# The first layer's output projection as seven quarter products, with its early weights in idle value buffers

## The chip, the core and the metric

The kernel runs on one core of one Trainium2 chip. The metric is device time in microseconds (us) of one execution; lower is better. The engines are TensorE (PE, matrix products), VectorE (DVE), ScalarE (ACT), GpSimd (POOL) and SyncE (SP, which issues most DMAs). They run asynchronously, each through its own instruction list in a fixed order, and wait for each other by semaphores. An instruction that waits holds up all that stands behind it on its engine.

## What is computed

An encoder trunk of two layers over 512 tokens of width 1024. Layer 0 mixes tokens by a neighbourhood attention, layer 1 by a latent attention; each has 16 heads, a SiLU gate z on the branch, an output projection, a residual add, and a gated embedding with a second 1024x1024 product.

```
def mixer_na(xn, w_in, rpb, w_out):
    q, k, v, z = jnp.split(xn @ w_in, 4, axis=-1)
    o = neighbourhood_attention(q, k, v, rpb)          # heads split and joined
    return (o.reshape(B, S, hd) * jax.nn.silu(z)) @ w_out
...
for each layer:  x = x + mixer(rmsnorm(x));  x = x + p * sigmoid(rmsnorm(x) @ gate)
```

All is fp32. A product is made of three terms on high and low parts (hi*hi, lo*hi, hi*lo), each a chain of matmuls on 128x128 by 128x512 tiles. A weight piece of 128x1024 is loaded raw, ACT copies its high part, and POOL or DVE subtracts to make its low part.

## The kernel before

Work is written with a scheduler that fixes the order on each engine from the dependences; pools of buffers (tags with a number of copies) decide when a load may start, and an instruction can be told to stand behind another (`issue_after`).

- **First attention** (about 100 to 241 us). `attend(j, also)` handles head pair j: scores, softmax, transposes, value products; `gated` multiplies the pair's output u by z on POOL and splits it into `oh` and `ol`. In each of the 16 heads `sum_step` issues one DMA of POOL's queue that adds two quarters of a gate weight in DRAM: 8 for the first layer's gate, 8 for the second's. The last three z products (`NLATE`) run between the last heads.
- **Output projection** (`out_proj`, 222 to 276 us). Two halves n of the columns by four token tiles t: eight products of 24 matmuls. Weights come by `load_w`; low parts go to POOL, or for every second piece to DVE. As soon as a product is added to the residual `r`, `turn_h` scales it, transposes it and hands it to `keep_half`, which makes the gate's operands.
- **Gate** (`gate_seven`, 276 to 317 us). Seven quarter products (Strassen's scheme with sums of weights and of operands) in the order 1, 7, 2, 6, 5, 3, 4, each of 24 matmuls. `prep(p)` loads and splits its two weight pieces; POOL makes all their low parts (L796).
- **Second layer.** The same with the latent attention (401 to 555 us); there POOL normalises each softmax tile `ex` (L1056) before PE transposes it.

Between projection and gate, raw weights share three `wraw` buffers, high and low parts three of `whi` and `wlo` each and ten of `w4`. PSUM has banks by tags T, O, S and mm, two each.

## Time and profile before

| | |
|---|---|
| median of 3 runs | 653.7 us (652.97 to 653.79) |
| the profiled execution | 653.56 us, of it 651.5 us span, mean granted PE clock 0.995 |
| PE busy | 640.2 us, 98% |
| ACT, DVE, POOL busy | 453.4, 427.7, 408.4 us |
| first attention's last value product | starts its successor at 241.49 us |
| output projection and gate | to about 276 us, to about 317 us |

Busy time of PE is the time in which at least one matmul is under way. A window row gives for a stretch of the span the busy time and the count of each engine. A group row gives line, engine, operation, tiles and shape, then busy time and mean duration in ns, then the idle time right before its instructions and what ended it. A timeline row gives start, duration and, in brackets, the idle time before.

### The profile page before, as it was taken

The page shows a single profiled execution, that of the slowest core. Times are in us where ns is not written, and L with a number is a line of the kernel's source. Part 1 is how long each engine was busy: PE and PEld are TensorE (multiplying, and loading weights), DVE is VectorE, ACT ScalarE, POOL GpSimd, SP SyncE. Part 2 cuts the span into 40 slices and gives each one's busy share as a digit, 9 for nine tenths or more (in the row PEclk, how much of TensorE's full clock was granted, in tenths as well). Part 3 has the DMA queues.
Part 4 walks back from the last instruction along what each step waited for, and adds up shares of the span by engine and source line. Part 5 has one row for each costly group of instructions (what it writes and reads, how often), then busy time and mean ns, then how long its engine had stood idle before and what let it go on. Part 6 is the DMA issues. An engine that isn't in the chain of part 4 may idle for free.

```text
span 651.5 us, 9980 instructions
## 1 busy us (share of the span) xinstructions
PE 640.2 (98%) x3299; PEld 541.9 (83%) x3299; DVE 427.7 (66%) x886; ACT 453.4 (70%) x903; POOL 408.4 (63%) x371
## 2 busy tenths in 40 slices
...
GB/s 326 355 124 306 217 66 179 263 205 217 229 209 217 239 178 342 147 154 188 224 140 102 78 109 156 32 75 24 49 50 66 65 84 112 229 292 126 193 65 162
DMA packets 46131, 107.41 MB, mean 165 GB/s; under 512 B 4736, under 2 KB 17792, under 8 KB 46080
## 3 DMA queue, kind: packets, MB, share of 16 engines
...
## 4 chain that ended last, share of the span: by engine, by line
PE 83%; POOL 1%; ACT 1%; DVE 0%; DMA 0%; issue 0%; POOLq 0%
PE ps_mm L123 27%; PE ps_S L123 10%; PE ps_mm L959 7%; PE ps_T L155 6%; PE ps_T L851 5%; PE ps_O L1071 5%; PE ps_mm L851 3%; PE ps_S L851 3%; PE ps_O L608 2%; PE ps_T L123 2%; PE ps_O L123 2%; PE ps_mm L909 2%; PE ps_T L301 2%; PE ps_T L596 2%; PE ps_S L909 1%; PE ps_S L559 1%
## 5 line engine op out<-in xcount | busy, mean ns | idle before, releaser
L101 POOL TENSOR_TENSOR wwlo<-wraw,wwhi 128x1024 fp32r<-128x1024 f32 (+5 forms) x68 | 122.3, 1810 | 93.5 <-ACT wwhi L100 41.9
L796 POOL TENSOR_TENSOR wlo<-wraw,whi 128x512 fp32r<-128x512 f32 x56 | 72.7, 1331 | 22.3 <-ACT whi L794 20.2
L1056 POOL TENSOR_TENSOR ex<-ex,rc 128x512 f32<-128x512 f32 x64 | 66.2, 1043 | 26.6 <-DVE rc L1055 22.5
L100 ACT ACTIVATE wwhi<-wraw 128x1024 fp32r<-128x1024 f32 (+5 forms) x71 | 55.1, 799 | 34.3 <-PE ps_mm L123 18.9
L1054 ACT ACTIVATE ex<-ps_S,mx 128x512 f32<-128x512 f32 x64 | 44.0, 687 | 12.6 <-DVE mx L1052 10.9
L1052 DVE TENSOR_REDUCE mx<-ps_S 128x1 f32<-128x512 f32 x64 | 43.7, 683 | 8.4 <-PE ps_S L123 7.7
L582 POOL TENSOR_TENSOR ex<-ex,rc 128x128 f32<-128x128 f32 (+1 forms) x64 | 37.5, 701 | 17.7 <-DVE rc L578 17.5
L112 DVE TENSOR_TENSOR pt_lo<-ps_T,pt_hi 128x512 fp32r<-128x512 f32 x64 | 43.1, 680 | 7.1 <-ACT pt_hi L110 6.7
L110 ACT ACTIVATE pt_hi<-ps_T 128x512 fp32r<-128x512 f32 x64 | 37.7, 594 | 3.4 <-PE ps_T L155 3.0
L155 PE MATMUL ps_T<-ident,ex 128*128 128x128 f32 x256 | 38.3, 272 | 0.0
L155 PEld LDWEIGHTS ps_T<-ident,ex 128*128 128x128 f32 x256 | 31.5, 140 | 7.5
L123 PE MATMUL ps_mm<-xh,wwhi 128*128 128x512 f32 x120 | 33.7, 404 | 0.0
L221 DVE TENSOR_TENSOR u<-ps_O,u 64x512 f32<-64x512 f32 x32 | 21.9, 685 | 17.7 <-ACT u L220 17.2
L576 ACT ACTIVATE ex<-ex,mx 128x128 f32<-128x128 f32 (+1 forms) x64 | 30.2, 473 | 4.2 <-DVE mx L565 4.1
L123 PE MATMUL ps_mm<-xl,wwhi 128*128 128x512 f32 x120 | 31.9, 395 | 0.0
L794 ACT ACTIVATE whi<-wraw 128x1024 fp32r<-128x1024 f32 x28 | 29.3, 1057 | 3.2 <-DMA wraw<-sum 2.4
L123 PE MATMUL ps_mm<-xh,wwlo 128*128 128x512 f32 x120 | 31.1, 394 | 0.0
L123 PE MATMUL ps_S<-ke,qe 96*128 96x512 f32 x96 | 28.9, 407 | 0.3 <-DMA qe<-rl 0.3
L123 PE MATMUL ps_S<-ko,qo 128*128 128x512 f32 x96 | 28.9, 409 | 0.0
L959 PE MATMUL ps_mm<-cT,wwhi 128*128 128x512 f32 x94 | 27.7, 393 | 0.0
L220 ACT ACTIVATE u<-ps_O 64x512 f32<-64x512 f32 x32 | 18.9, 591 | 12.0 <-PE ps_O L608 8.8
L225 POOL TENSOR_TENSOR u<-u,z 128x512 f32<-128x512 f32 x16 | 22.6, 1412 | 7.5 <-DVE u L221 7.5
...
## 6 DMA issues: line engine op xcount, KB each, us to landing
...
wraw<-na_qk SPq DMA_DIRECT2D x16, 512.0 KB, 4.9
wraw<-sum SPq DMA_DIRECT2D x16, 512.0 KB, 3.3
...
wraw<-gate SPq DMA_DIRECT2D x12, 512.0 KB, 3.3
wraw<-na_v SPq DMA_DIRECT2D x10, 512.0 KB, 3.4
...
wraw<-na_o SPq DMA_DIRECT2D x8, 512.0 KB, 4.8
```

Source lines behind the costliest of these rows:

```text
L100: nc.scalar.activation(hi[:, c], raw[:, c], AF.Copy)
L101: f = lambda e, c=c: e.tensor_tensor(out=lo[:, c], in0=raw[:, c], in1=hi[:, c].bitcast(F32), op=ALU.subtract)
L110: self.last_copy = self.act.activation(hi, src, AF.Copy, scale=scale)
L112: self.dve.tensor_tensor(out=lo, in0=src, in1=hi.bitcast(F32), op=ALU.subtract)
L123: last = self.last_mm = nc.tensor.matmul(out, l, r, start=i == 0, stop=i == n - 1)
L155: self.last_mm = self.nc.tensor.transpose(t[:, i * P:(i + 1) * P], b, self.ident)
L796: nc.gpsimd.tensor_tensor(out=lo[:, o], in0=raw[:, o], in1=hi[:, o].bitcast(F32), op=ALU.subtract)
L851: mm = nc.tensor.matmul(ps, l, r, start=j == 0 and p in banks, stop=j == 11 and p in (2, 3, 4), skip_group_check=True)
L959: self.last_mm = nc.tensor.matmul(PS[key], *terms[i], start=i == 0, stop=i == len(terms) - 1)
L1052: nc.vector.reduce_max(mx, sp, axis=AX.X, negate=True)
L1054: nc.scalar.activation(ex, sp, AF.Exp, bias=mx, accum_out=sm)
L1056: nc.gpsimd.tensor_tensor(out=ex, in0=ex, in1=rc.to_broadcast([P, S]), op=ALU.mult)
```

## The change

The first layer's output projection becomes `out_seven`: seven quarter products in the order 1, 7, 2, 4, 6, 5, 3, each of two token tiles with 12 matmuls. Products 2, 4, 5 and 3 accumulate on the banks of 1, 7, 6 and 6. Each result is added to or subtracted from one to three halves of the residual tiles. `gated_seven` multiplies u into z and forms sums and differences of z's halves on DVE: those for products 1 and 7 (head pairs 0 to 3) and 2 and 4 (pairs 4 to 7) become the operands `oh`, `ol`; those for 6, 5 (`Y`) and 3 (`Y3`) are split by ACT and DVE in `out_seven`. The sums of its weights (products 4 to 7) are made in DRAM in the first eight heads, the gate's in the other eight; the second layer's gate sums move into the second attention, one in each of heads 1 to 8, behind a normalisation.

`piece_of` loads one weight piece, 14 in all. `places` says where it goes: `w` is the ring of three, `v` the `w4` ring (now 8), `0` and `1` are two of the first attention's value buffers, now in a pool `seam`, that are free once their values are used. Products 1 and 7 are loaded from head pair 5 on. All low parts are POOL's but the second pieces of products 2 and 4, which DVE makes. The residual loads move into `out_seven`, behind `gp`. Transposes of odd tiles use bank O, the last late z bank S. The gate's order becomes 1, 7, 6, 2, 5, 3, 4, and `keep_mixed` makes its operands.

The orders below are taken behind the last attention head. First PE. Before, at the matmuls behind the last value product (`ww` is the fourth weight piece, `oh_1001` and `ol_1003` the operands of head pairs 4 to 7):

```order
L123 MATMUL ps_mm<-wwhi,ol_1002 128x512 x2
L123 MATMUL ps_mm<-wwlo,oh_1000 128x512 x2
L123 MATMUL ps_mm<-wwhi,oh_1001 128x512 x2
L123 MATMUL ps_mm<-wwhi,ol_1003 128x512 x2
L123 MATMUL ps_mm<-wwlo,oh_1001 128x512 x2
L123 MATMUL ps_S<-wwlo,oh_1001 128x512 x2
L123 MATMUL ps_S<-wwhi,ol_1003 128x512 x2
L123 MATMUL ps_S<-wwlo,oh_1001 128x512 x2
L123 MATMUL ps_mm<-ww_2617,oh_1001 128x512 [waits Activation_49]
L123 MATMUL ps_mm<-ww_2617,oh_1001 128x512
L123 MATMUL ps_mm<-ww_2617,ol_1003 128x512
L123 MATMUL ps_mm<-ww_2617,ol_1003 128x512 [waits Pool_49]
```

And now, from the last two value products (`ps_O`) on; `ps_mm` is product 7, `ps_T` product 2 on product 1's bank, `oh_1008` the operands of head pairs 4 to 7:

```order
L617 MATMUL ps_O<-ph,Q_510 128x256
L617 MATMUL ps_O<-pl,Q_510 128x256
L824 MATMUL ps_mm<-whi,oh_1007 128x512 x2
L824 MATMUL ps_mm<-whi,ol_1009 128x512 x2
L824 MATMUL ps_mm<-wlo,oh_1007 128x512 x2
L824 MATMUL ps_mm<-whi,oh_1007 128x512 x2
L824 MATMUL ps_mm<-whi,ol_1009 128x512 x2
L824 MATMUL ps_mm<-wlo,oh_1007 128x512 x2
L824 MATMUL ps_mm<-whi,oh_1007 128x512 x2
L824 MATMUL ps_mm<-whi,ol_1009 128x512 x2
L824 MATMUL ps_mm<-wlo,oh_1007 128x512 x2
L824 MATMUL ps_T<-whi,oh_1008 128x512 [waits DVE_49,Activation_49]
```

Before, 26 matmuls stand between the last value product and the first row that waits for the last head's operand; now 18 stand between it and product 2, whose first matmul waits for DVE and ACT. DVE's list at that place now (`Yl` is a low part of a Y operand, `wlo` the low part of product 2's second piece, the rows with `ps_T` are the adds of product 1; the last two read its first tile):

```order
L760 TENSOR_TENSOR z<-z 128x256 [waits DVE_49]
L802 TENSOR_TENSOR Yl<-z,Yh 128x512 [waits Activation_49]
L752 TENSOR_TENSOR wlo<-wraw,whi 128x512 [waits DMAHW7_49,Activation_49]
L752 TENSOR_TENSOR wlo<-wraw,whi 128x512
L833 TENSOR_TENSOR r<-r,ps_T 128x512 [waits DMAHW4_49]
L760 TENSOR_TENSOR z<-z 128x256 [waits Pool_49]
L833 TENSOR_TENSOR r<-r,ps_T 128x512 [waits DMAHW5_49]
L805 TENSOR_TENSOR Y_2687<-z,Y_2687 128x256 [waits Activation_49]
L833 TENSOR_TENSOR r<-r,ps_T 128x512 [waits DMAHW6_49]
L831 TENSOR_TENSOR r<-ps_T,r 128x512
```

Before, DVE had at that place only the last head's `u` and two low parts of weights. The second place is ACT and SP. ACT before, from the last head's evacuation `u<-ps_O` (L220) on:

```order
L220 ACTIVATE u<-ps_O 64x512 [waits PE_49]
L228 ACTIVATE oh_1001<-u 128x512 [waits Pool_49]
L100 ACTIVATE ww_2617<-wraw 128x1024 [waits DMAHW5_49]
L100 ACTIVATE ww_2777<-wraw 128x1024 [waits DMAHW6_49]
L100 ACTIVATE ww_2783<-wraw 128x1024 [waits DMAHW7_49]
L100 ACTIVATE ww_2789<-wraw 128x1024 [waits DMAHW5_49]
L100 ACTIVATE ww_2795<-wraw 128x1024 [waits DMAHW6_49]
```

And now, from the same evacuation (L227) on; `w_2737` is product 6's first piece, the two `whi` are product 2's:

```order
L227 ACTIVATE u<-ps_O 64x512 [waits PE_49]
L750 ACTIVATE w_2737<-wraw 128x1024 [waits DMAHW2_49]
L769 ACTIVATE oh_1008<-z 128x512 [waits Pool_49]
L750 ACTIVATE whi<-wraw 128x1024 [waits DMAHW6_49]
L801 ACTIVATE Yh<-z 128x512 [waits DVE_49]
L750 ACTIVATE whi<-wraw 128x1024 [waits DMAHW7_49,Activation_49]
L804 ACTIVATE Y_2687<-z 128x256 [waits DVE_49]
```

A weight's high part now stands between the evacuation and the last head's operand. SP before, around the residual loads:

```order
L99 DMA wraw<-na_o 128x1024 [waits DMAHW2_49,DVE_49,Activation_49]
L99 DMA wraw<-na_o 128x1024 [waits DMAHW3_49,Pool_49]
L1251 DMA r<-x 128x1024 [waits DMAHW0_49,PE_49]
L1251 DMA r<-x 128x1024 [waits DMAHW1_49,PE_49]
L1251 DMA r<-x 128x1024 x2
L148 DMA gp<-ple_norm 128x1024 [waits DMAHW4_49]
L99 DMA wraw<-na_o 128x1024 [waits DMAHW5_49,DVE_49]
L99 DMA wraw<-na_o 128x1024 [waits DMAHW6_49,Pool_49]
```

And now; `sumout_106` holds the weights of product 4, `sumout_108` of product 6:

```order
L748 DMA wraw<-sumout_106 128x1024 [waits DMAHW0_49,Activation_49,Pool_49]
L748 DMA wraw<-sumout_108 128x1024 [waits DMASW6_49,DMAHW1_49,DVE_49,Activation_49]
L155 DMA gp<-ple_norm 128x1024 [waits DMAHW3_49,DMASW1_49,PE_49]
L794 DMA r<-x 128x1024 [waits DMAHW4_49]
L794 DMA r<-x 128x1024
L794 DMA r<-x 128x1024 [waits DMAHW6_49]
L794 DMA r<-x 128x1024 [waits DMAHW7_49]
L748 DMA wraw<-sumout_108 128x1024 [waits DMAHW2_49,Activation_49,Pool_49]
```

The residual loads have moved behind product 4's second and product 6's first piece; the first of these waits for POOL, the second for DVE. The third place is POOL, before, from the last but one pair's `u` on:

```order
L225 TENSOR_TENSOR u<-u,z 128x512 [waits DVE_49]
L229 TENSOR_TENSOR ol_1003<-u,oh_1001 128x512 [waits Activation_49]
L101 TENSOR_TENSOR wwlo<-wraw,wwhi 128x1024 [waits DMAHW3_49,PE_49,Activation_49]
L225 TENSOR_TENSOR u<-u,z 128x512 [waits DVE_49]
L229 TENSOR_TENSOR ol_1003<-u,oh_1001 128x512 [waits Activation_49]
L101 TENSOR_TENSOR ww_2778<-wraw,ww_2777 128x1024 [waits DMAHW6_49,Activation_49]
L101 TENSOR_TENSOR ww_2790<-wraw,ww_2789 128x1024 [waits DMAHW5_49,PE_49,Activation_49]
```

And now; the first `wlo` is product 4's first piece, `w_2737` product 6's first, the second `wlo` product 2's first:

```order
L759 TENSOR_TENSOR z<-u,z 128x512 [waits DVE_49]
L752 TENSOR_TENSOR wlo<-wraw,whi 128x512 [waits DMAHW0_49,PE_49,Activation_49]
L752 TENSOR_TENSOR wlo<-wraw,whi 128x512
L770 TENSOR_TENSOR ol_1010<-z,oh_1008 128x512 [waits Activation_49] x2
L759 TENSOR_TENSOR z<-u,z 128x512 [waits DVE_49]
L752 TENSOR_TENSOR w_2737<-wraw,w_2737 128x512 [waits DMAHW2_49,PE_49,Activation_49]
L752 TENSOR_TENSOR w_2737<-wraw,w_2737 128x512
L770 TENSOR_TENSOR ol_1010<-z,oh_1008 128x512 [waits Activation_49]
L752 TENSOR_TENSOR wlo<-wraw,whi 128x512 [waits DMAHW6_49,PE_49,Activation_49]
L752 TENSOR_TENSOR wlo<-wraw,whi 128x512
```

The low part of product 4 waits for PE: its buffer was read last by the late z product of the last head pair. Product 6's low part has moved ahead of the last head's operand `ol`.

The diff:

```diff
-                l, step = divmod(j, 4)
-                if step == 0:
-                    self.quarters(l)
-                attend(j, lambda e: self.sum_step(l, 2 * step + e))
+                key = (("out", 0), ("gate", 0))[j // 4]
+                if j == 5:
+                    self.places = list("01wwvvw01vvwwv") + list("vw0v1vwwvvw0v1")
+                    self.out_early(None, 0, oT)
+                attend(j, lambda e: self.sum_step(key, 2 * (j % 4) + e))
...
             late = range(8 - NLATE, 8)
             zs.update(self.z_phase(a["na_z"], xT, late, self.last_exp.ins))
             for j in late:
-                self.gated(U[j], zs[j], oT, j)
+                gate(U[j], zs, oT, j)
...
+    def sum_step(self, key, i):
 
         p, src, add = ((7, "f", 0), (6, 1, 0), (7, 3, 1), (4, 2, 0), (6, 7, 1), (5, 1, 0), (4, 6, 1), (5, "f", 1))[i]
-        src = self.sums[layer][src] if src in (6, 7) else self.quarter[layer][src]
-        self.nc.gpsimd.dma_start(self.sums[layer][p], src, accum_op=ALU.add if add else ALU.bypass, max_dma_last_dim=1024)
+        src = self.sums[key][src] if src in (6, 7) else self.quarter[key][src]
+        self.nc.gpsimd.dma_start(self.sums[key][p], src, accum_op=ALU.add if add else ALU.bypass, max_dma_last_dim=1024)
+
+    def piece_of(self, pool, key, p, c, after=None, rest=None):
+        place = self.places.pop(0)
+        src = self.quarter[key][p] if p < 4 else self.sums[key][p]
+        raw = self.wp.tile([P, 1024], F32, name="wraw", tag="wraw", bufs=3)
+        if place in "01":
+            both = self.seam.tile([P, 2, 1024], F32R, name="w" + place, tag=f"Q{place}0", bufs=1)
+            hi, lo = both[:, 0, :], both[:, 1, :]
+        else:
+            q, n, tags = (self.wp, 3, ("whi", "wlo")) if place == "w" else (pool, self.wxn, ("w4", "w4"))
+            hi, lo = (q.tile([P, 1024], F32R, name=n0, tag=t, bufs=n) for n0, t in zip(("whi", "wlo"), tags))
+        self.last_load = nc.sync.dma_start(raw, src[c * P:(c + 1) * P])
+        with self.tc.issue_after(after.ins) if after else nullcontext():
+            self.act.activation(hi, raw, AF.Copy)
+        for o in (slice(0, S), slice(S, 2 * S)):
+            (rest or nc.gpsimd).tensor_tensor(out=lo[:, o], in0=raw[:, o], in1=hi[:, o].bitcast(F32), op=ALU.subtract)
+        return hi, lo
+
+    def gated_seven(self, u, zs, oT, j):
+
+        nc = self.nc
+        z = zs[j]
+        nc.gpsimd.tensor_tensor(out=z, in0=u, in1=z, op=ALU.mult)
+        sub = lambda o, x, y: nc.vector.tensor_tensor(out=o, in0=x, in1=y, op=ALU.subtract)
+        g, k = divmod(j, 4)
+        hi, lo = (oT[s][g][:, k, :] for s in range(2))
+        if g == 0:
+            sub(u[:, HI], z[:, LO], z[:, HI])
+            for x, c in ((z, LO), (u, HI)):
+                nc.scalar.activation(hi[:, c], x[:, c], AF.Copy)
+                nc.gpsimd.tensor_tensor(out=lo[:, c], in0=x[:, c], in1=hi[:, c].bitcast(F32), op=ALU.subtract)
+            return
+        nc.scalar.activation(hi, z, AF.Copy)
+        nc.gpsimd.tensor_tensor(out=lo, in0=z, in1=hi.bitcast(F32), op=ALU.subtract)
+        y = zs[k]
+        sub(y[:, HI], y[:, HI], z[:, HI])
+        sub(y[:, LO], y[:, LO], y[:, HI])
+        sub(z[:, LO], z[:, LO], y[:, LO])
+
+    def out_early(self, pool, layer, oT):
+
+        key = "out", layer
+        self.W = {}
+        self.oT = oT
+        for p in (1, 7):
+            self.W[p] = [self.piece_of(pool, key, p, c) for c in range(2)]
+
+    def out_seven(self, pool, layer, zs, res, after, last_mm):
+
+        nc = self.nc
+        key = "out", layer
+        oT, W = self.oT, self.W
+        order = (1, 7, 2, 4, 6, 5, 3)
+        C = {}
+        prep = lambda p: W.__setitem__(p, [self.piece_of(pool, key, p, c, rest=nc.vector if c and p in (2, 4) else None)
+                                           for c in range(2)])
+        for t in range(NT):
+            nc.sync.dma_start(res[t], self.a["x"][t] if layer == 0 else self.spill[t])
+        for p in order[2:4]:
+            prep(p)
+        Y = [self.bigtile(f"Y{s}") for s in "hl"]
+        Y3 = self.bigtile("Y3")
+        y3 = [Y3[:, 2 * s:2 * s + 2, :].rearrange("p a (b c) -> p (a b) c", b=2) for s in range(2)]
+        for k in range(4):
+            nc.scalar.activation(Y[0][:, k, :], zs[k], AF.Copy)
+            nc.vector.tensor_tensor(out=Y[1][:, k, :], in0=zs[k], in1=Y[0][:, k, :].bitcast(F32), op=ALU.subtract)
+        for k in range(4):
+            nc.scalar.activation(y3[0][:, k, :], zs[4 + k][:, LO], AF.Copy)
+            nc.vector.tensor_tensor(out=y3[1][:, k, :], in0=zs[4 + k][:, LO], in1=y3[0][:, k, :].bitcast(F32),
+                                    op=ALU.subtract)
+        src = {1: ([x[0] for x in oT], 0), 7: ([x[0] for x in oT], 256), 2: ([x[1] for x in oT], 0),
+               4: ([x[1] for x in oT], 256), 6: (Y, 0), 5: (Y, 256), 3: (y3, 0)}
+        banks = {1: "T", 7: "mm", 6: "S"}
+        home = {2: 1, 4: 7, 5: 6, 3: 6}
+        mm = last_mm
+        for n, p in enumerate(order):
+            if 0 < n < 4:
+                prep(order[n + 3])
+            x, o = src[p]
+            for i in range(2):
+                if p in banks:
+                    C[p, i] = self.psum(banks[p])
+                ps = C[home.get(p, p), i]
+                m = [(x[s][:, k, o + i * P:o + (i + 1) * P], W[p][k // 2][r][:, k % 2 * S:(k % 2 + 1) * S])
+                     for c in range(2) for s, r in ((0, 0), (1, 0), (0, 1)) for k in (2 * c, 2 * c + 1)]
+                for j, (l, r) in enumerate(m):
+                    with self.tc.issue_after(mm):
+                        self.last_out = nc.tensor.matmul(ps, l, r, start=j == 0 and p in banks,
+                                                         stop=j == 11 and p in (2, 4, 3), skip_group_check=True)
+                    mm = self.last_out.ins
+                for t, h, op in {1: ((0, 1, 0), (2, 1, 0), (2, 0, 1)), 7: ((2, 1, 0),), 2: ((0, 0, 1),), 4: ((2, 0, 1),),
+                                 6: ((2, 0, 0),), 5: ((2, 1, 1),), 3: ((0, 1, 1),)}[p]:
+                    r = res[t + i][:, h * S:(h + 1) * S]
+                    if op:
+                        nc.vector.tensor_tensor(out=r, in0=ps, in1=r, op=ALU.add)
+                    else:
+                        nc.vector.tensor_tensor(out=r, in0=r, in1=ps, op=ALU.subtract)
+                if p in (2, 6, 5, 3):
+                    after(t + i, h)
...
-        mm = self.last_out
-        order = (1, 7, 2, 6, 5, 3, 4)
+        mm, loaded = self.last_out, self.last_load
+        order = (1, 7, 6, 2, 5, 3, 4) if layer in MIXED else (1, 7, 2, 6, 5, 3, 4)
...
-            if p == 6:
+            if p == 6 and layer not in MIXED:
                 self.mixed(3)
...
-                    elif p == 2 and i and layer == 0:
+                    elif p == 2 and i and layer == 0 and layer not in MIXED:
                         kept.append((i, 0, ps))
                     elif p == 2:
                         finish(i, 0, ps, last=True)
...
-            nc.gpsimd.tensor_tensor(out=ex, in0=ex, in1=rc.to_broadcast([P, S]), op=ALU.mult)
+            norm = nc.gpsimd.tensor_tensor(out=ex, in0=ex, in1=rc.to_broadcast([P, S]), op=ALU.mult)
+            step = h - 1
+            if qt == 1 and 0 <= step < 8:
+                with self.tc.issue_after(norm.ins):
+                    self.sum_step(("gate", 1), step)
...
-        ctx2 = ExitStack()
+        ctx2, ctx3 = ExitStack(), ExitStack()
+        self.seam = ctx3.enter_context(tc.tile_pool(name="seam", bufs=1, reuse_waits="tile"))
         nav = ctx2.enter_context(tc.tile_pool(name="nav", bufs=1, reuse_waits="tile"))
-        shared = lambda name, tag, d, shape: nav.tile(shape, d, name=name, tag=tag, bufs=1)
+        shared = lambda name, tag, d, shape: (self.seam if tag[2] == "0" else nav).tile(shape, d, name=name, tag=tag, bufs=1)
...
-                self.out_proj(a["na_o"] if layer == 0 else a["mla_o"], oT, res, turn_h, last)
+                if mixed:
+                    self.out_seven(pool, layer, zs, res, turn_h, last)
+                else:
+                    self.out_proj(a["na_o"] if layer == 0 else a["mla_o"], oT, res, turn_h, last)
```

98 lines of the change are left out of this document (62 added, 36 removed).

## The prediction

> **What bounds the kernel now.** I read the head of the page first, then the chain that ended last, then windows over the first layer's output projection and gate.
>
> ```profile
> span 651.5 us, 9980 instructions
> ...
> PE 640.2 (98%) x3299; PEld 541.9 (83%) x3299; DVE 427.7 (66%) x886; ACT 453.4 (70%) x903; POOL 408.4 (63%) x371
> ...
> PE 83%; POOL 1%; ACT 1%; DVE 0%; DMA 0%; issue 0%; POOLq 0%
> 242.00:276.00 34.00, 34.00 (x159) 28.28 (x158) 18.95 (x22) 17.60 (x25) 20.37 (x14) 1.00 0.69 251
> 276.00:317.00 41.00, 41.00 (x194) 34.21 (x193) 32.71 (x56) 34.61 (x62) 34.38 (x30) 1.00 0.57 182
> ```
>
> TensorE (PE) is busy 640.2 of 651.5 us, and no other engine has more than 1% of the chain. The window rows give span, PE, PE loads, DVE, ACT, POOL: through the projection (242 to 276) and the gate behind it (276 to 317) PE has no idle time at all, while DVE, ACT and POOL stand idle for 40 to 48% of the projection. So two things count: matmuls that go, at their full price, and every wait that PE newly meets, also at its full price. The profiled execution took 653.56 us, 2.06 more than its span and 0.14 below the median of 653.7; the sum below starts from 653.56.
>
> **What goes.** The old projection has 8 products of 24 matmuls 128x512, 192 in all; seven quarter products of 24 make 168. The program's count of such matmuls falls by the same 24.
>
> ```profile
> 240.57 0.25 PE L608 MATMUL ps_O<-ph,Q 128*128 128x192 f32 x1
> ...
> 241.49 0.63 PE L123 MATMUL ps_mm<-wwlo,oh 128*128 128x512 f32 x2
> ...
> 247.41 0.61 PE L123 MATMUL ps_mm<-ww,oh 128*128 128x512 f32 x2
> ```
>
> From 241.49 to 247.41 there are 26 matmuls of that shape, 0.2277 us each by their starts. 24 of them are 5.46 us, all on PE, all on the path: **-5.5 us**. The gate keeps its seven products of 24; only their order and two operand copies change, and the copies sit on engines with idle time.
>
> **What comes, and where it bites.** The place is the seam behind the last attention head. Before, the chain there is this:
>
> ```profile
> 241.69 0.59 ACT L220 ACTIVATE u<-ps_O 64x512 f32<-64x512 f32 x1 [5.31 <-PE ps_O L608]
> 242.31 0.69 DVE L221 TENSOR_TENSOR u<-ps_O,u 64x512 f32<-64x512 f32 x1 [6.15 <-ACT u L220]
> 243.09 1.28 POOL L225 TENSOR_TENSOR u<-u,z 128x512 f32<-128x512 f32 x1 [4.82 <-DVE u L221]
> 244.40 0.63 ACT L228 ACTIVATE oh<-u 128x512 fp32r<-128x512 f32 x1 [2.12 <-POOL u L225]
> 245.11 1.30 POOL L229 TENSOR_TENSOR ol<-u,oh 128x512 fp32r<-128x512 f32 x1 [0.74 <-ACT oh L228]
> ```
>
> The last value product starts its successor at 241.49, the last operand is ready at 246.41, and PE asks for the first half of it only at 247.41, because 26 matmuls that need nothing new stand between. In the new PE order only 18 stand there, the rest of product 7, worth 18 x 0.2277 = 4.1 us. Then comes product 2, which accumulates on product 1's banks and therefore waits until DVE has added product 1's first tile to three residual halves. I count that chain from the end of the last value product as time 0 and go through the queues in the order they now have. Prices:
>
> ```profile
> L796 POOL TENSOR_TENSOR wlo<-wraw,whi 128x512 fp32r<-128x512 f32 x28 | 36.1, 1318 | 12.0 <-ACT whi L794 11.2 <-POOL wlo L796 0.7
> L100 ACT ACTIVATE ww<-wraw 128x1024 fp32r<-128x1024 f32 x5 | 5.1, 1051 | 4.5 <-DMA wraw<-na_o 4.5
> L741 ACT ACTIVATE X<-ps_T 128x512 fp32r<-128x512 f32 x1 | 0.6, 598 | 6.3 <-PE ps_T L155 6.3
> L653 DVE TENSOR_TENSOR wlo<-wraw,whi 128x512 fp32r<-128x512 f32 x6 | 3.8, 688 | 4.3 <-ACT whi L652 4.3
> L635 DVE TENSOR_TENSOR r<-ps_mm,r 128x512 f32<-128x512 f32 x2 | 1.3, 686 | 1.8 <-PE ps_mm L123 1.8
> DMA to landing us min/median/max: 3.1/3.5/6.5
> DMA to landing us min/median/max: 3.5/3.6/5.1
> r<-x SPq DMA_DIRECT2D x4, 512.0 KB, 5.5
> ```
>
> The first landing row is for all weight pieces from 236 to 320 us, the second for the three of the old projection in the crowd of residual loads.
>
> 1. The low part of product 4's first piece takes the buffer that the last late z product still reads, so it cannot start before that product ends. From there to time 0 PE has 30 matmuls 128x512, and 23 transposes and value products. The eight value products from 240.57 to 241.49 give 0.115 for one: 30 x 0.2277 + 23 x 0.115 = 9.5, less some 0.2 until the product's end is seen: **-9.3**. Two POOL halves of 36.1/28 = 1.29 end at -6.7.
> 2. Only then may SP load product 4's second piece (the raw buffer is the same): 3.5, -3.2. ACT makes its high part, 1.05, -2.1; DVE its low part, 2 x 0.69, -0.8. With five handovers of up to 0.1, the gaps between the rows above, **about -0.2**.
> 3. SP's next load, product 6's first piece, takes that raw buffer again, so it is issued at -0.2, followed by the norm gains and the four residual tiles: 5.1 in such a crowd, about 5.0. The residuals, issued within 2 us behind it, land by 7.5 at 5.5 us each, so they are not last.
> 4. ACT's next instruction after the evacuation of the last head is the high part of this piece. It waits at the head of the queue, and behind it stand the last operand, product 2's first high part, a Y operand and product 2's second high part: 1.05 + 0.63 + 1.05 + 0.60 + 1.05 = 4.4, to **9.4**.
> 5. DVE, in order: the low part of product 2's second piece, 1.4 alone; then four adds of product 1 at 0.69 (three of its first tile, one of the second between them) and two 128x256 operations, half of that each: 3.5.
>
> ```profile
> 246.02 1.47 DVE L101 TENSOR_TENSOR ww<-wraw,ww 128x1024 fp32r<-128x1024 f32 x1 [3.01 <-ACT ww L100]
> 247.91 2.92 DVE L101 TENSOR_TENSOR ww<-wraw,ww 128x1024 fp32r<-128x1024 f32 x1 [0.42 <-ACT ww L100]
> 247.01 2.74 POOL L101 TENSOR_TENSOR ww<-wraw,ww 128x1024 fp32r<-128x1024 f32 x1 [0.60 <-ACT ww L100]
> ```
>
> The same DVE work took 1.47 us with POOL idle and 2.92 beside a POOL operation of the same kind. From 6 to 13 POOL will be at such work here (low part, last operand, low part), so the low part costs 1.4 to 2.9; I take 2.2, since one of its halves may find POOL between two. The adds end at 9.4 + 2.2 + 3.5 = **15.1**. POOL's own low part of product 2 is through at about 12.7 by 2 x 1.29 + 1.30 + 2 x 1.29 from 6.2, so the adds are last.
>
> PE is there at 4.1: **it waits 11.0 us**. Ends: with both loads at 3.5 and the low part at 1.4 it is 8.6; with 5.1 and 6.5 for the loads and 2.9 it is 14.7. What would be late next is nothing near: during such a wait the pieces of products 6 and 5 get ahead, and POOL's 5.2 us for two pieces is below 24 x 0.2277 = 5.5 for a product.
>
> A stop that long has a price of its own:
>
> ```profile
> 0.76 4.85 PE L1187 MATMUL ps_T<-const-bfloat16-1.0 128*128 128x512 bf16 x11 [0.76 <-PEq L1464]
> ...
> 6.61 0.40 PE L673 MATMUL ps_mm<-whi 128*128 128x512 f32 x1
> 6.84 0.39 PE L673 MATMUL ps_mm<-wlo,whi 128*128 128x512 f32 x1
> ...
> 642.39 0.40 PE L851 MATMUL ps_O<-wlo,X 128*128 128x256 f32 x2
> ...
> 644.00:646.00 2.00, 0.00 (x0) 0.00 (x0) 1.79 (x7) 1.23 (x3) 1.03 (x2) 0.69 0.58 216
> 646.00:648.00 2.00, 0.00 (x0) 0.00 (x0) 0.85 (x2) 0.72 (x1) 0.51 (x1) 0.50 0.64 236
> ```
>
> PE's last matmul ends at 642.8; the granted clock (third number from the end) averages 0.69 in the window from 644, so it fell to 0.50 at about 644.8, 2 us after PE stopped. At the kernel's start the first eleven matmuls stand (5.26 - 0.76)/11 = 0.41 us apart, and the spacing 0.23 is reached at 6.61, 5.9 us after the first. So after an 11 us stop PE should start at half pace. If that lasts as long as at the start, half of 5.9, 2.9 us, is lost; if the clock rises as fast as it fell, 1.0. I take the middle, **+1.9 us**.
>
> The Trainium skill, "TensorE: Matmul & The Clock Gate", section "What's actually happening", says that an idle window of about 3.4 us halves the clock and a busy one of the same length restores it; by that the loss would be about 1.7 us, an estimate from the page, and the sum 0.2 lower. The drop at the end of this trace agrees in kind.
>
> **The eight sums in the second attention.** They move from POOL's queue in the first attention, whose slots out's sums now take, into the second.
>
> ```profile
> 193.62 1.34 POOL L730 DMA_DIRECT2D sum<-gate  x1
> 194.42 2.96 POOL L101 TENSOR_TENSOR wwlo<-wraw,wwhi 128x1024 fp32r<-128x1024 f32 x1
> L1056 POOL TENSOR_TENSOR ex<-ex,rc 128x512 f32<-128x512 f32 x64 | 66.2, 1043 | 26.6 <-DVE rc L1055 22.5 <-PE ps_S L123 2.4 <-PE ps_O L1071 1.6
> ```
>
> An issue holds POOL 0.8 us before the next instruction starts. Eight are 6.4 us; POOL's idle time ahead of the normalisations there is 26.6 us in 64 steps, so I cost them at nothing. Uncovered, what is queued behind is the next normalisation, whose transposes PE waits for: at most 6.4.
>
> **Sum:** 653.56 - 5.5 + 11.0 + 1.9 = **661.0 us**.
>
> **Rivals.**
> - *The seam is covered.* If PE reaches product 2 after the adds, 24 matmuls are the whole effect: 653.56 - 5.5 = 648.1, faster. For it: before, the last head's operand was ready 1.0 us ahead of its need, and PE never stopped. It decides at 4.1 us: the adds would have to be done by then, 11 us earlier than counted, that is without the two loads in row. Chance 0.12.
> - *Half of it.* Links overlap more than I count, for one because PE itself arrives later at the seam than the matmul count says, while the load chain started on time. With 2 to 7 us of wait and 0 to 1.9 of slow clock: 650 to 657. Chance 0.15.
> - *The sums bite as well.* 8 x 0.8 uncovered in the second attention, or low parts in POOL's queue delaying the last heads of the first: 661.0 + 3 to 6.4 = 664 to 667. Chance 0.1.
> - My forecast, a wait of 8.6 to 14.7 with 1.0 to 2.9 for the slow clock: 657.7 to 665.7. Chance 0.63.
>
> **Range and chances.** 654 to 665 leaves out the covered seam, the lower half of the half case and most of the last rival. Faster by over 0.2% (below 652.4; 0.2% is about what a measurement of this kernel can tell from no change) is the covered seam and the lower third of the half case: 0.17. Within 0.2%: 0.06. Slower: 0.77.
>
> **What the new profile would show.** Right: one idle stretch of PE of 9 to 14 us between product 7 and product 2, put down to DVE's residual adds, the DVE before them waiting for ACT's high parts and ACT for the load of product 6's first piece; the granted clock at half in and just after it; PE's busy matmul count down by 24. Wrong: PE busy through the seam, or its idle time put down to POOL or to the residual loads, or idle stretches in the second attention behind the sums. I am wrong by most if the low part of product 4's first piece doesn't wait for the late z product, for then the whole load chain moves up by several us.

## The result, and the profile after

The changed kernel is slower: **677.05 us** (median of four runs, 674.9 to 679.59) beside 653.56 for the kernel before on the same chip, a ratio of 1.0362 with an interval of 1.0325 to 1.04. The profiled execution took 674.9 us, 673.1 of it span, and is the fastest of the four. The direction was forecast; 661.0 and the range up to 665 were not enough.

The head of the page, the list of what PE waited for (total, times, longest), a window of the first attention and three windows inside the stretches in which the granted clock was 0.50 (span, PE, PE loads, DVE, ACT, POOL, granted clock, DMA share, GB/s), all of the kernel after:

```profile
span 673.1 us, 10016 instructions
PE 642.8 (95%) x3275; PEld 539.8 (80%) x3275; DVE 461.0 (68%) x920; ACT 464.6 (69%) x921; POOL 442.5 (66%) x403
PE ps_T L824 <- DVE r L831: 9.3, 1, 9.3
PE ps_T L824 <- DVE pl L119: 5.1, 1, 5.1
PE ps_O L617 <- DVE u L228: 2.3, 1, 2.3
PE ps_T L967 <- DVE ps_T L946: 1.1, 1, 1.1
...
PE ps_O L617 <- DVE pl L119: 0.7, 1, 0.7
PE ps_mm L130 <- ACT wwhi L107: 0.6, 1, 0.6
180.00:200.00 20.00, 16.82 (x90) 14.21 (x91) 13.06 (x40) 17.40 (x41) 18.96 (x22) 0.93 0.70 233
...
197.20:200.50 3.30, 2.96 (x12) 2.68 (x12) 1.74 (x9) 3.28 (x10) 3.30 (x7) 0.50 0.34 106
245.00:248.30 3.30, 3.30 (x8) 2.62 (x9) 2.78 (x6) 0.80 (x2) 0.00 (x0) 0.50 0.00 0
258.70:268.80 10.10, 3.52 (x8) 2.81 (x9) 8.79 (x12) 3.48 (x4) 8.34 (x7) 0.50 0.70 240
```

The matmul count is down by 24, from 3299 to 3275, as it should be. What came in is read as two sums. **Idle time of PE** (span less busy) went from 651.5 - 640.2 = 11.3 us to 673.1 - 642.8 = 30.3: 19.0 more. The list names it: 9.3 ahead of product 2, 5.1 ahead of product 1's second tile (its bank T is not free), 2.3 + 0.7 + 0.6 = 3.6 inside the first attention, 1.1 in the gate; together 19.1. Only the first was in the forecast. **Busy time of PE** should have fallen by 5.5 and rose by 2.6, which is 8.1 us too much. In the three stretches at half clock, where the kernel before had 1.00, PE was busy 2.96 + 3.30 + 3.52 = 9.8 us, and half of that, 4.9, is about what the clock cost. The other 3.2 us came almost all at full clock, in small pieces that do not count as idle time; where they come from is not shown. So 19.0 + 8.1 - 5.5 = 21.6 = 673.1 - 651.5.

The stop ahead of product 2 ends as the forecast had it, with the low part on DVE and the adds behind it. First PE's rows around it in the kernel after (start, duration, what it is, how many together, and in brackets the idle time before), then the load that ACT waits for, then two of DVE's rows that lead there:

```profile
251.55 0.28 PE L617 MATMUL ps_O<-pl,Q 128*128 128x256 f32 x1
...
255.33 0.61 PE L824 MATMUL ps_mm<-wlo,oh 128*128 128x512 f32 x2
265.28 1.19 PE L824 MATMUL ps_T<-whi,oh 128*128 128x512 f32 x2 [9.34 <-DVE r L831]
...
268.83 0.65 PE L824 MATMUL ps_T<-whi,ol 128*128 128x512 f32 x2
```

```profile
253.88 1.06 ACT L750 ACTIVATE w<-wraw 128x1024 fp32r<-128x1024 f32 x1 [1.41 <-DMA wraw<-sumout]
```

```profile
258.23 3.37 DVE L752 TENSOR_TENSOR wlo<-wraw,whi 128x512 fp32r<-128x512 f32 x2
...
264.45 0.68 DVE L831 TENSOR_TENSOR r<-ps_T,r 128x512 f32<-128x512 f32 x1
```

The last value product ends at 251.83, PE has no more to do from 255.9, 4.1 later as counted, and the last add ends at 265.13, 13.3 after that product against 15.1 in the forecast. Two operations of the low part took 3.37 us beside POOL, where 1.4 to 2.9 was allowed; the load of product 6's first piece was in 2.1 us after that product, where 5.0 was counted. So the load held ACT by little: ACT made the last operand at 254.85, 0.3 after POOL had its input ready at 254.55. Behind the stop the first eight matmuls take 268.83 - 265.28 = 3.55 us, against 8 x 0.2277 = 1.82 at the usual pace: 1.7 lost.

The stop of 5.1 was not forecast. PE waits for DVE to read the last head's transposes out of bank T (`pl`, L119). PE's row of the kernel after, DVE's queue ahead of it, and POOL's rows beside it and beside product 2's adds:

```profile
244.96 1.22 PE L824 MATMUL ps_T<-w,oh 128*128 128x512 f32 x2 [5.13 <-DVE pl L119]
...
248.48 0.63 PE L824 MATMUL ps_T<-w,ol 128*128 128x512 f32 x2
```

```profile
234.12 3.12 DVE L802 TENSOR_TENSOR Yl<-z,Yh 128x512 fp32r<-128x512 f32 x1
...
242.82 1.50 DVE L760 TENSOR_TENSOR z<-z 128x256 f32<-128x256 f32 x1
244.34 0.56 DVE L119 TENSOR_TENSOR pl<-ps_T,ph 128x384 fp32r<-128x384 f32 x1
...
246.01 0.67 DVE L802 TENSOR_TENSOR Yl<-z,Yh 128x512 fp32r<-128x512 f32 x1
246.61 0.41 DVE L760 TENSOR_TENSOR z<-z 128x256 f32<-128x256 f32 x1
```

```profile
233.67 3.01 POOL L759 TENSOR_TENSOR z<-u,z 128x512 f32<-128x512 f32 x2
...
242.77 1.26 POOL L770 TENSOR_TENSOR ol<-z,oh 128x512 fp32r<-128x512 f32 x1 [1.54 <-ACT oh L769]
...
264.48 2.52 POOL L752 TENSOR_TENSOR wlo<-wraw,whi 128x512 fp32r<-128x512 f32 x2 [1.76 <-ACT whi L750]
```

The same instruction Yl lasts 3.12 us while POOL works and 0.67 at 246.01, when POOL is idle; a 128x256 subtraction lasts 1.50 and 0.41. The first ends at 237.24, 0.56 after the two POOL operations of 233.67; the other at 244.32, 0.29 after POOL's of 242.77: DVE stands until POOL lets go. The add of 264.45, which reads PSUM, takes its 0.68 though POOL is at work from 264.48 on. So in these rows it is DVE's operations with all operands in SBUF that are held. PE's first matmul of product 1's second tile stands behind that queue, and the first eight behind this stop take 248.48 - 244.96 = 3.52 us, 1.7 too many again.

The longest stop inside the first attention, 2.3 us up to 196.38, has the same look. A row of DVE in the kernel after, and POOL's beside it:

```profile
192.85 2.24 DVE L760 TENSOR_TENSOR u<-z 128x256 f32<-128x256 f32 x1
```

```profile
192.44 2.37 POOL L108 TENSOR_TENSOR wwlo<-wraw,wwhi 128x1024 fp32r<-128x1024 f32 x1
```

This subtraction is one that `gated_seven` adds. It took 2.24 us where 0.41 is usual and ended at 195.09, 0.28 after POOL's operation; the evacuation `u` (L228) that PE waits for stands behind it on DVE.

### The profile page after: what moved, and what is told of

Same layout as the page of the kernel before. It is cut to its first block, busy times and chain, and to the rows that moved or that the text cites. A ratio compares the mean times of both kernels' runs of the same rounds, so it can differ in the third digit from the quotient of the medians.

```text
span 673.1 us, 10016 instructions
## 1 busy us (share of the span) xinstructions
PE 642.8 (95%) x3275; PEld 539.8 (80%) x3275; DVE 461.0 (68%) x920; ACT 464.6 (69%) x921; POOL 442.5 (66%) x403
## 4 chain that ended last, share of the span: by engine, by line
PE 63%; ACT 6%; DVE 5%; POOL 5%; DMA 4%; issue 2%; SPq 0%; POOLq 0%; ACTq 0%; DVEq 0%
PE ps_mm L130 20%; PE ps_S L130 7%; PE ps_mm L1075 5%; PE ps_T L162 5%; PE ps_O L1191 4%; PE ps_T L967 3%; POOL wlo L752 3%; PE ps_S L967 2%; PE ps_mm L1025 2%; PE ps_T L308 2%; PE ps_mm L967 2%; DMA wraw<-gate 2%; PE ps_O L617 1%; PE ps_S L1025 1%; PE ps_T L605 1%
## 5 line engine op out<-in xcount | busy, mean ns | idle before, releaser
L108 POOL TENSOR_TENSOR wwlo<-wraw,wwhi 128x1024 fp32r<-128x1024 f32 (+5 forms) x66 | 117.9, 1813 | 90.4 <-PE ps_T L308 40.1
L752 POOL TENSOR_TENSOR wlo<-wraw,whi 128x512 fp32r<-128x512 f32 x66 | 88.2, 1368 | 18.4 <-ACT whi L750 17.0
L1172 POOL TENSOR_TENSOR ex<-ex,rc 128x512 f32<-128x512 f32 x64 | 70.6, 1155 | 18.2 <-DVE rc L1171 10.7
L107 ACT ACTIVATE wwhi<-wraw 128x1024 fp32r<-128x1024 f32 (+5 forms) x68 | 51.9, 787 | 28.9 <-PE ps_mm L130 13.1
L119 DVE TENSOR_TENSOR pt_lo<-ps_T,pt_hi 128x512 fp32r<-128x512 f32 x64 | 43.1, 681 | 7.9 <-ACT pt_hi L117 7.6
L750 ACT ACTIVATE whi<-wraw 128x1024 fp32r<-128x1024 f32 x34 | 35.6, 1056 | 11.8 <-DMA wraw<-sumout 4.2
L130 PE MATMUL ps_mm<-xh,wwhi 128*128 128x512 f32 x112 | 30.6, 402 | 0.6 <-ACT wwhi L107 0.6
L130 PE MATMUL ps_mm<-xh,wwlo 128*128 128x512 f32 x112 | 29.3, 402 | 0.0
L228 DVE TENSOR_TENSOR u<-ps_O,u 64x512 f32<-64x512 f32 x32 | 21.9, 684 | 7.3 <-ACT u L227 6.9
L119 DVE TENSOR_TENSOR pl<-ps_T,ph 128x384 fp32r<-128x384 f32 (+1 forms) x32 | 19.3, 618 | 7.8 <-ACT ph L117 7.6
L130 PEld LDWEIGHTS ps_mm<-xh,wwlo 128*128 128x128 f32 x112 | 21.0, 194 | 4.4
```

What stands on the lines that cost most here:

```text
L107: nc.scalar.activation(hi[:, c], raw[:, c], AF.Copy)
L108: f = lambda e, c=c: e.tensor_tensor(out=lo[:, c], in0=raw[:, c], in1=hi[:, c].bitcast(F32), op=ALU.subtract)
L119: self.dve.tensor_tensor(out=lo, in0=src, in1=hi.bitcast(F32), op=ALU.subtract)
L130: last = self.last_mm = nc.tensor.matmul(out, l, r, start=i == 0, stop=i == n - 1)
L752: (rest or nc.gpsimd).tensor_tensor(out=lo[:, o], in0=raw[:, o], in1=hi[:, o].bitcast(F32), op=ALU.subtract)
L1172: norm = nc.gpsimd.tensor_tensor(out=ex, in0=ex, in1=rc.to_broadcast([P, S]), op=ALU.mult)
```

## The experiments

Each kernel starts from the changed one unless its text says so, and was timed in four runs beside the kernel before, which stood between 652.77 and 653.1 us on those chips. "p2" is PE's wait ahead of product 2, "T" its wait ahead of product 1's second tile. Both are read from the one profiled execution of a kernel; as executions of one kernel differ by 1.5 to 7.4 us, a shift of a microsecond or two in such a wait is not shown by it alone.

### One stop at a time

**banks**: product 1 in the S banks, product 6 in T.

```diff
-        banks = {1: "T", 7: "mm", 6: "S"}
+        banks = {1: "S", 7: "mm", 6: "T"}
```

> Change: product 1 accumulates in the S banks and product 6 in the T banks (before: the other way round); nothing else. The changed kernel waits 5.1 us ahead of product 1's second tile, for a T bank that DVE frees. Theory A (the stalls stand one behind another): that wait goes, and because the last head's value products, the last operand and product 6's loads hang behind product 1, all of it moves up. A shorter wait of 2 to 3 us for the same DVE copies appears ahead of the last value products, product 2 still waits 8 to 11 us, and the time falls by 3 to 6 us, to 671 to 674. Rival B (the chain of loads behind product 2 stands fixed in time): the wait only moves, product 2 waits 13 to 15 us, and the time stays within 1.5 us of 677.

677.86 us, 1.0379 (1.0351 to 1.0408): no gain. T is gone, p2 9.5, and PE now waits elsewhere, by the list of its waits in this run:

```profile
PE ps_O L617 <- DVE u L228: 9.9, 2, 7.6
PE ps_S L824 <- DVE r L831: 9.5, 1, 9.5
```

With product 1 let through, the value products behind it meet the same late DVE queue and stop for 7.6 us. The bank was only the place where the lag of DVE showed.

**early6**: out's first four pieces are prepared from head pair 6 on, not from head pair 5.

```diff
-                if j == 5:
+                if j == 6:
```

> Change: the pieces of products 1 and 7 are prepared from head 6 on (before: head 5); nothing else. The changed kernel idles PE for about 5.6 us between 176 and 197 us, where POOL works 10 of 10 us, partly at these pieces' low parts. Theory A (POOL's low parts there delay DVE and POOL work that PE waits for): the idle time between 160 and 220 us falls to under 2 us, and the time falls by 3 to 6 us, to 671 to 674. Rival B (the same POOL and DVE work only comes later, where there is even less room): the idle time appears between 200 and 245 us instead, and the time is within 2 us of 677 or above it.

669.52 us, 1.0245 (1.0216 to 1.0274): the largest gain of a single edit. Its window from 180 to 200, the stretch in which the changed kernel had POOL busy 18.96 of 20 us:

```profile
180.00:200.00 20.00, 20.00 (x111) 17.00 (x110) 15.04 (x37) 16.62 (x39) 17.30 (x22) 1.00 0.64 211
```

PE has no idle time there, and the clock is full. In exchange p2 rose to 11.8, and a wait of 2.1 appeared at 215.6; T fell to 2.6. In sum PE's idle time in the profiled executions is 669.7 - 640.6 = 29.1 us, 1.2 less than in the changed kernel, and its busy time 2.2 less. The two medians differ by 7.5 us, the two profiled executions by 3.4 (674.9 and 671.5, the fastest of one kernel and the slowest of the other), so the size of the gain is known only to some 3 us. That there is a gain is clear, as the two intervals of the ratio (1.0216 to 1.0274 and 1.0325 to 1.04) do not touch.

**y_late**: the last heads' combinations for products 6, 5 and 3 wait until product 1's adds are through.

```diff
-        sub(y[:, HI], y[:, HI], z[:, HI])
-        sub(y[:, LO], y[:, LO], y[:, HI])
-        sub(z[:, LO], z[:, LO], y[:, LO])
+        self.y_work.append(lambda: (sub(y[:, HI], y[:, HI], z[:, HI]), sub(y[:, LO], y[:, LO], y[:, HI]),
+                                    sub(z[:, LO], z[:, LO], y[:, LO])))
...
+                if (p, i) == (1, 1):
+                    y_all(add)
```

> Change: the subtractions and splits that make the operands Y and Y3 of products 6, 5 and 3 come behind the additions of product 1 on DVE and ACT (before: ahead of them, as each head is gated); POOL's work stays. Theory O (the order in DVE's queue holds PE at the T bank and ahead of product 2): the wait for the T bank falls from 5.1 to under 1.5 us, the wait ahead of product 2 from 9.3 to 5 to 8; the work that went comes back as a new wait ahead of product 6, of 2 to 8 us, for Yh or Yl, and the time falls by 2 to 6 us. Rival R (the loads hold it): the waits at the T bank and ahead of product 2 stay as they are, and the time rises by the wait ahead of product 6.

677.01 us, 1.0366 (1.0351 to 1.0382): the same time, with other stops.

```profile
PE ps_T L827 <- DVE r L834: 10.6, 1, 10.6
PE ps_T L162 <- DVE hg L1399: 3.6, 1, 3.6
```

T is gone (5.1), p2 grew by 1.3 and 3.6 us came up behind the projection, where the norm waits for DVE, which has the postponed work ahead of it.

**dve_seam**: POOL's part of the gating of head pairs 5 to 7, and the low parts of products 2, 4, 6, 5 and 3, go to DVE.

```diff
-        nc.gpsimd.tensor_tensor(out=z, in0=u, in1=z, op=ALU.mult)
+        (nc.vector if j > 4 else nc.gpsimd).tensor_tensor(out=z, in0=u, in1=z, op=ALU.mult)
...
-        nc.gpsimd.tensor_tensor(out=lo, in0=z, in1=hi.bitcast(F32), op=ALU.subtract)
+        (nc.vector if j > 4 else nc.gpsimd).tensor_tensor(out=lo, in0=z, in1=hi.bitcast(F32), op=ALU.subtract)
...
-        prep = lambda p: W.__setitem__(p, [self.piece_of(pool, key, p, c, rest=nc.vector if c and p in (2, 4) else None)
+        prep = lambda p: W.__setitem__(p, [self.piece_of(pool, key, p, c, rest=nc.vector)
```

> Change: at the seam POOL's subtractions and products go to DVE: the low parts of the pieces of products 2, 4, 6, 5 and 3 (seven halves of the fourteen were POOL's for the first two products, all of them for the others), and gating product and low part of heads 5 to 7. Theory L (a DVE operation with both operands in SBUF stands still while POOL works in SBUF; in the changed kernel one of 128x512 took 3.12 us at 234.1, and 0.67 at 246.0 with POOL idle): DVE's operations between 230 and 265 us take 0.4 and 0.7 us again although there are more of them, the wait for the T bank falls from 5.1 to under 1.5 us, the one ahead of product 2 from 9.3 to 4 to 6, and the time by 7 to 11 us, to 666 to 670. Rival Q (DVE is late because it has too much to do): with some 15 operations more it is later still, both waits grow, and the time rises to 680 or more.

675.39 us, 1.0341 (1.0318 to 1.0364). DVE in the same stretch, with more work on it:

```profile
236.87 1.29 DVE L802 TENSOR_TENSOR Yl<-z,Yh 128x512 fp32r<-128x512 f32 x2
...
238.67 0.42 DVE L805 TENSOR_TENSOR Y<-z,Y 128x256 fp32r<-128x256 f32 x1
```

The durations are back at 0.65 for 128x512 and 0.42 for 128x256, and T fell from 5.1 to 1.1: the long ones came from POOL, as they are gone with its work although DVE does more. But p2 was 9.8, not smaller, and the time fell by 1.7 us only. So p2 does not hang on the long durations alone: DVE, which now has more to do, works from 251.91 to the end of the adds at 260.68 without a pause.

### What holds product 2

**r_first**: SP issues the residual tiles ahead of the loads of product 4's second and product 6's first piece.

```diff
-        self.last_load = nc.sync.dma_start(raw, src[c * P:(c + 1) * P])
+        with self.tc.issue_after(self.res_load.ins) if key[0] == "out" and (p, c) in ((4, 1), (6, 0)) else nullcontext():
+            self.last_load = nc.sync.dma_start(raw, src[c * P:(c + 1) * P])
...
+            self.res_load = nc.sync.dma_start(res[t], self.a["x"][t] if layer == 0 else self.spill[t])
```

> Change: SP issues the four residual loads ahead of the load of product 4's second piece and of product 6's first piece, which are held behind them; with it the high parts of these two pieces come behind product 2's on ACT. The prediction's chain (step 3 and 4) has the load of product 6's first piece at the head of ACT's queue as the cause of 5 to 6 us of the wait ahead of product 2. Theory P (the prediction): without it that wait falls from 9.3 to 3 to 5 us, and the time by 4 to 7. Theory A: in the run the load landed only 0.3 us behind the last operand's need, so it costs little now; the wait is set by the last operand, the slow low parts on DVE and the adds behind them. Then the wait falls to 7.5 to 9 us and the time by 0.5 to 2.

678.96 us, 1.04 (1.0375 to 1.0426): p2 8.1, T 7.2, 2 us more in the gate. The loads are out of ACT's way here, and p2 is only 1.2 us shorter: in the changed kernel they held product 2 by little. Why T is longer is open.

**adds_first**: as r_first, and the low part of product 2's second piece stands behind the adds.

```diff
+            low = lambda o=o: (rest or nc.gpsimd).tensor_tensor(out=lo[:, o], in0=raw[:, o], in1=hi[:, o].bitcast(F32), op=ALU.subtract)
+            if key[0] == "out" and (p, c) == (2, 1):
+                self.held.append(low)
...
+                while (p, i) == (1, 0) and self.held:
+                    with self.tc.issue_after(add.ins):
+                        self.held.pop(0)()
```

> Change: that of r_first, and the low part of product 2's second piece comes behind the four additions of product 1's first tile on DVE (before: ahead of them). Theory A: the additions no longer wait for high and low parts of that piece, 3.4 us on DVE beside POOL, so product 2 starts 4 to 5 us earlier than in the changed kernel; the low part itself is then next and takes back up to 1 us. Idle time of PE at product 2 falls from 9.7 to 4 to 6 us, the time by 4 to 6 us. Rival B: product 2 then waits for its own low parts on POOL and DVE as long as before (9 us), and the time stays within 1.5 us of r_first.

678.91 us, 1.0398 (1.0374 to 1.0421): p2 6.9, T 6.6. The wait is shorter and the time is not: what p2 gives back, T and the gate take.

**dve_seam6**: dve_seam and early6 together, so that all stops ahead of the seam should be gone.

```diff
-                if j == 5:
+                if j == 6:
...
-        prep = lambda p: W.__setitem__(p, [self.piece_of(pool, key, p, c, rest=nc.vector if c and p in (2, 4) else None)
+        prep = lambda p: W.__setitem__(p, [self.piece_of(pool, key, p, c, rest=nc.vector)
```

> Change: dve_seam and early6 together, nothing else. Theory: the stall of the first attention (early6: 7.5 us of the median) and the T bank's (dve_seam: 4 us of idle time) are separate causes and add, as far as the wait ahead of product 2, 9 to 12 us in both, lets them: 664 to 668. Rival: the wait ahead of product 2 takes up what the other saves, and the time is that of early6, 669 to 671.

669.34 us, 1.0238 (1.0212 to 1.0263). T is 1.3, the first attention lost 2.1 in one stop, and p2 rose to 14.6. PE's wait in the list, then ACT ahead of it:

```profile
PE ps_T L824 <- DVE r L831: 14.6, 1, 14.6
```

```profile
248.96 1.06 ACT L750 ACTIVATE w<-wraw 128x1024 fp32r<-128x1024 f32 x1 [4.52 <-DMA wraw<-sumout]
250.03 0.59 ACT L227 ACTIVATE u<-ps_O 64x512 f32<-64x512 f32 x1
```

ACT stands for 4.52 us on a load of a summed piece and only then, at 250.03, evacuates the last head, whose value products had ended at 246.10. This is the forecast's mechanism, a load at the head of ACT's queue with the last head behind it, one place earlier than counted; 14.6 us stand against an upper end of 14.7. In the changed kernel PE came later to the seam, and ACT waited 1.41 us for that load.

**dve_seam6r**: the same with r_first's edit.

> Change against dve_seam6: SP's residual loads go ahead of the loads of product 4's second and product 6's first piece (as r_first did to the changed kernel). In dve_seam6 ACT stood 4.52 us at the head of its queue for the load of product 6's first piece, and the last head's evacuation, operand and product 2's high parts stood behind it; PE waited 14.56 us. Theory P (the prediction's steps 1 to 4: this chain of loads holds ACT, once nothing else does): that wait of ACT goes, the wait ahead of product 2 falls from 14.6 to 5 to 8 us, and the time from 669.3 to 660 to 664. Rival: as in r_first the wait falls by under 2 us only, and the time stays above 667.

666.87 us, 1.0198 (1.0174 to 1.0223), the fastest of all variants. ACT's evacuation of the last head waits for PE instead of a load, and PE's waits from 180 to 300 us are these:

```profile
247.82 0.59 ACT L227 ACTIVATE u<-ps_O 64x512 f32<-64x512 f32 x1 [6.33 <-PE ps_O L617]
```

```profile
PE ps_T L825 <- DVE r L832: 8.2, 1, 8.2
PE ps_S L567 <- DVE mx L577: 2.0, 1, 2.0
PE ps_T L825 <- DVE pl L119: 1.9, 1, 1.9
PE ps_S L825 <- DVE r L832: 1.5, 1, 1.5
PE ps_S L825 <- ACT whi L751: 1.1, 1, 1.1
```

Undoing one link (the loads ahead of the residuals in SP's queue) takes p2 from 14.6 to 8.2, so the load chain is shown for dve_seam6, not for the changed kernel, where the same edit gave 1.2 (r_first). Of the 6.4 us, 3.9 are ACT's late evacuation; the rest lies in DVE's queue, where dve_seam6 has one more low part between the adds and waits 0.5 for residual tiles. The time fell by 2.5 us, within what the two intervals leave open: 1.5 + 1.1 + 0.6 of new waits stand against the 6.4, and PE's busy time was 642.8 instead of 639.7 in the profiled executions.

**ds6ra**: dve_seam6r with adds_first's edit.

> Change against dve_seam6r: the low part of product 2's second piece comes behind the four additions of product 1's first tile on DVE (as adds_first did to r_first). Theory: 1.3 us of DVE's work go from ahead of the additions, product 2 starts 1.0 to 1.3 us earlier, the low part is in time for its seventh matmul or nearly, and the time is 0.5 to 1.5 us below dve_seam6r. Rival: product 2 then waits as long for the low part, and the time is the same within 0.5 us.

668.09 us, 1.0229 (1.0208 to 1.025): p2 7.0, T 2.8, and 2.3 in bank S behind it. No gain beyond the scatter.

**own_bank**: product 2 gets banks of its own, so that it need not wait for the adds.

```diff
-        banks = {1: "T", 7: "mm", 6: "S"}
-        home = {2: 1, 4: 7, 5: 6, 3: 6}
+        banks = {1: "T", 7: "mm", 2: "S", 6: "T"}
+        home = {4: 7, 5: 6, 3: 6}
...
-                for t, h, op in {1: ((0, 1, 0), (2, 1, 0), (2, 0, 1)), 7: ((2, 1, 0),), 2: ((0, 0, 1),), 4: ((2, 0, 1),),
+                for t, h, op in {1: ((0, 0, 1), (0, 1, 0), (2, 1, 0), (2, 0, 1)), 7: ((2, 1, 0),), 2: ((0, 0, 1),), 4: ((2, 0, 1),),
```

> Change against the changed kernel: product 2 no longer accumulates on product 1's T banks but starts in the S banks, product 6 takes the T banks, the transposes of the gate's input take S in place of T, and DVE adds product 1 to the first half of tiles 0 and 1 as well (two operations of 0.7 us more). So product 2 needs no addition of product 1 any longer. Theory P (the prediction: the additions are what PE waits for): PE starts product 2 when its first high and low part are there, some 4 to 6 us earlier against the last value product; the wait ahead of product 2 falls from 9.3 to 3.5 to 5.5, a wait of up to 2 us for its second low part follows, and the time falls by 3 to 5 us. Rival S (the last head's operand and the low parts are as late as the additions): the wait only changes its name, stays above 8 us in sum, and the time stays within 1.5 us of 677.

683.77 us, 1.047 (1.0448 to 1.0493).

```profile
PE ps_T L824 <- DVE pl L119: 6.5, 1, 6.5
PE ps_S L162 <- DVE hg L1394: 6.0, 1, 6.0
PE ps_S L824 <- POOL wlo L752: 3.8, 2, 3.0
```

Product 2 no longer waits for `r` but for its own weights, 3.8 us in two pieces for low parts and 0.3 for a high part: the adds were the gate, and 4.1 us is what its operands alone hold it, though T is 1.3 longer here. Later the norm's transposes wait 6.0 for their input `hg` from DVE; why it is late is not shown.

### What a stop costs behind it

**warm_p2r**: r_first with 32 more matmuls ahead of product 2, on tiles that are there, into a bank that nobody reads.

```diff
+        self.warmers = {(2, 0): 32}
...
+                if (p, i) in self.warmers:
+                    spare = self.psum("S")
+                    for j in range(self.warmers[p, i]):
+                        with self.tc.issue_after(mm):
+                            mm = nc.tensor.matmul(spare, oT[0][0][:, 0, :P], W[1][0][0][:, :S], start=True, stop=True).ins
```

> Change against r_first: PE runs 32 matmuls 128x512 more, whose result nobody reads, in the wait ahead of product 2 (7.3 us of the 8.3 us in which PE stood idle); engine orders up to product 4 are those of r_first. Theory K (the stop itself costs clock): in r_first the first 12 matmuls behind the stop stand 0.43 us apart instead of 0.2277, about 2.5 us; here they stand 0.23 apart from the first one on, and the time is 2 to 3 us below r_first although 32 matmuls are added. Rival W (the slow matmuls wait for operands one by one): they stay 0.43 us apart, and the time is that of r_first within 1 us.

678.10 us, 1.0373 (1.0352 to 1.0393). PE in this run, and then in r_first, at the same place:

```profile
260.13 7.41 PE L826 MATMUL ps_S<-w,oh 128*128 128x512 f32 x32
268.45 0.70 PE L831 MATMUL ps_T<-whi,oh 128*128 128x512 f32 x2 [0.90 <-DVE r L838]
268.99 0.62 PE L831 MATMUL ps_T<-whi,ol 128*128 128x512 f32 x2
```

```profile
265.47 1.19 PE L825 MATMUL ps_T<-whi,oh 128*128 128x512 f32 x2 [8.05 <-DVE r L832]
...
270.73 0.73 PE L825 MATMUL ps_T<-whi,oh 128*128 128x512 f32 x2
```

With PE kept at work the first pairs behind take 0.70 and 0.62; behind the bare stop twelve matmuls take 270.73 - 265.47 = 5.26 us, against 2.73 at the usual pace: 2.5 lost. So the slow start belongs to the stop. The total fell by 0.9 us only, which the intervals don't tell from nothing: less 7.3 us for the 32 matmuls PE's busy time is 643.2, against 643.0 in r_first. So what was saved at product 2 was lost elsewhere; the granted clock from 200 to 220 us, for one, is 0.93 in this run and 1.00 in r_first.

### Putting them together

**best1**: early6, r_first, dve_seam and y_late in one kernel.

> Change: four edits together: pieces of products 1 and 7 from head 6 on (as in early6), SP's residual loads ahead of product 4's second piece (as in r_first), the seam's low parts and gating on DVE (as in dve_seam), and Y and Y3 behind product 1's additions (as in y_late). Theory: the first attention loses under 3 us, the T bank under 1, product 2 waits 3 to 5 us (value products, gating, four low parts and one addition of the last head on DVE: some 8 us, less the 4.1 us of matmuls that PE has), product 6 waits for Y up to 4 us: 656 to 662. Rival: product 6 waits 8 us or more for Y because all of DVE's work now stands behind the additions: 664 to 670.

668.46 us, 1.0253 (1.0212 to 1.0295), no better than early6 alone. p2 is 6.6 and T 1.7; a wait of 5.6 has come up in the gate, and DVE's row there, beside a row of POOL operations without a gap from 304.62 to 317.60, shows why:

```profile
309.90 8.85 DVE L853 TENSOR_TENSOR X<-c,X 128x512 fp32r<-128x512 f32 x2
```

**best2**: best1, with the low parts of product 2 and of the operand of the gate's product 5 on POOL.

```diff
-                self.operand(p, i, (self.C if p == 5 else self.B)[i])
+                self.operand(p, i, (self.C if p == 5 else self.B)[i], self.nc.gpsimd if p == 5 else None)
```

> Change against best1: the low parts of product 2's two pieces go back to POOL, which stands idle there, and in the gate the low parts of product 5's operand go from DVE to POOL. In best1 the two operations of the latter took 8.85 us on DVE beside an unbroken row of POOL operations (1.4 us by the usual 0.7 each), and PE waited 5.57 us for them at 312.6. Theory L (DVE with both operands in SBUF stands still while POOL works): PE's wait at product 5 of the gate falls from 5.6 to under 1.5 us, with the additions 2.5 us earlier the wait ahead of product 2 falls from 6.6 to 4 to 5, and the time falls from 668.5 to 659 to 663. Rival: DVE's low part waits in POOL's queue instead, PE waits 4 us or more for it, and the time stays above 665.

670.34 us, 1.0264 (1.0216 to 1.0312). p2 is 3.8, but the standstill in the gate moved to another instruction and still costs PE 5.6. DVE, then POOL, in this run:

```profile
314.94 7.37 DVE L1460 TENSOR_TENSOR x1n<-r,gn 128x512 f32<-128x512 f32 x1
```

```profile
314.96 2.55 POOL L753 TENSOR_TENSOR wlo<-wraw,whi 128x512 fp32r<-128x512 f32 x2
317.47 2.53 POOL L753 TENSOR_TENSOR w<-wraw,w 128x512 fp32r<-128x512 f32 x2
319.94 1.81 POOL L108 TENSOR_TENSOR wwlo<-wraw,wwhi 128x768 fp32r<-128x768 f32 x1
```

One DVE operation with both operands in SBUF took 7.37 us, to 322.31, while POOL went through five operations without a gap, to 321.75.

**best4**: best2, with the low parts of four of the gate's fourteen pieces moved to DVE.

```diff
-            W[p] = [self.piece_of(pool, ("gate", layer), p, c, after) for c in range(2)]
+            W[p] = [self.piece_of(pool, ("gate", layer), p, c, after, nc.vector if layer == 0 and c and p in (2, 5, 3, 4) else None) for c in range(2)]
```

> Change against best2: in the first layer's gate the low parts of the second pieces of products 2, 5, 3 and 4 go from POOL to DVE, so that POOL's row of operations there has gaps; nothing else. In best2 that row went without a pause from 299.97 to 321.75, and a DVE operation 128x512 with both operands in SBUF that began at 314.94 took 7.37 us and ended 0.6 us behind the row's end; PE waited 5.58 us behind it. Theory L (such an operation stands still while POOL's row goes on): no DVE operation there takes over 3 us, PE's wait of 5.58 us falls below 2, and the time falls from 670 to 662 to 667. Rival M (DVE is late there because the norm's inputs are late): the wait stays above 4 us and the time at 668 or more.

674.00 us, 1.0312 (1.0282 to 1.0343). The wait of 5.6 is gone. From the norm to the gate PE now has six waits of 0.9 to 2.2 us for DVE and ACT, 9.8 together, where best2 had 5.6, 1.4, 0.9 and 0.9, 8.8 together.

**best3** is best2 with own_bank's edit, and **best5** is best4 with it and all transposes of the norm in O:

```diff
-                                         "O" if layer in MIXED and t % 2 else "T")
+                                         "O" if layer in MIXED else "T")
```

> Change: best2 and own_bank together. Theory: product 2 waits for its first high and low part alone, 1 to 3 us, and the second waits stay under 2 us in sum; 654 to 660. Rival: the work on DVE that used to run in that wait is then late for product 6, PE waits 3 us or more there, and the time is that of best2 within 1.5 us.

> Change: best4 with product 2 in banks of its own (S, product 6 in T, as in own_bank), and the transposes of the gate's input all in the O banks, so that none stands in product 2 behind a bank that product 2 itself holds. In own_bank this cost 6.0 us of wait for the gate's input. Theory: ahead of product 2 PE waits 1 to 3 us for high and low parts, no wait over 2 us comes within product 2, and the time is 4 to 7 us below best4. Rival: the two O banks now hold up the eight transposes one behind another, a wait of 4 us or more appears in the products behind, and the time is that of best4 within 2 us.

best3 took 676.20 us, 1.0359 (1.0329 to 1.0389): p2 3.1 in four pieces, and waits of 4.6 and 4.8 behind it. best5 took 691.26 us, 1.0609 (1.0566 to 1.0652), the slowest of all: PE waits 9.6 us in the gate for one operand `X` of ACT. That the two banks for all transposes are the cause is likely but not shown.

## Why the prediction was right in direction and wrong in size

The profiled execution lies 13.9 us above the 661.0 of the sum. By terms: -1.7 ahead of product 2 (9.3 for 11.0), +5.1 at T, +3.6 in the first attention, +1.1 in the gate, and +6.2 in PE's busy time (8.1 for 1.9); that is 14.3, and small differences make up the rest.

1. *"24 of them are 5.46 us"*: right. The count is down by 24, and no run speaks against the price.
2. *"it waits 11.0 us"* ahead of product 2: near in size, 9.3 for 11.0, and right in its last links. PE came at 4.1 as counted, and the adds were last; own_bank shows that they are the gate. The first links, two loads in a row, did not hold the changed kernel: ACT had its last high part at 258.19, 6.4 after the last value product and not 9.4, and r_first, without those loads in the way, still waits 8.1. The low part then took 3.37 for 2.2. These misses, -3.0 and +1.2, cancel in part, so the near number is partly luck. The loads do hold PE where the stops ahead of the seam are nearly gone: 14.6 in dve_seam6, and 8.2 with SP's order turned.
3. *"A stop that long has a price of its own"*, **+1.9**: one term for one stop, and there were several. Behind product 2's stop 1.7 was lost, near the term, and behind T's 1.7 again; the three stretches at half clock cost 4.9 together. PE's busy time is 8.1 us above what the count gives; the other 3.2, at full clock, were in no term. warm_p2r shows that the slow matmuls hang on the stop.
4. **The step that failed**: what was costed at nothing because it would run beside PE in other engines' idle time. The prediction read the cover from each engine's share of idle time (*"DVE, ACT and POOL stand idle for 40 to 48% of the projection"*) and charged the standstill of DVE beside POOL for a single low part, 2.2 us. That price was misread as well. Its row of 1.47 us was not with POOL idle (POOL worked until 246.41 and again from 247.01), and the one of 2.92 ended 1.08 behind POOL's operation, so that operation's end set it, not a factor of two. And the moved work lies ahead of the seam too: in the first attention POOL went to 18.96 of 20 us and PE stopped for 3.6, of it 2.3 behind a DVE subtraction that stood still beside POOL, and in the last heads' gating DVE's subtractions stood still beside POOL, which gave T's 5.1. early6 takes the first away by its time, dve_seam the second by its engine. The Trainium skill, "SBUF — State Buffer", section "SBUF: two separate sides", says that Vector and GpSimd share a pair of ports as a lock, and that a Vector operation with two SBUF inputs is fully blocked by a GpSimd one that started first, for a whole instruction. The rows agree that DVE stands still and that an add with one input in PSUM escapes (0.68 us); the 7.37 us beside five POOL operations are longer than one instruction.
5. The eight sums in the second attention, *"so I cost them at nothing"*: right to 0.4 us. The one wait that came in there is 0.4, at 486.1, for POOL's `ex`.
6. *The rival "The sums bite as well"* came nearest, by its half "low parts in POOL's queue delaying the last heads of the first", but at 3 to 6.4 us and 0.1 of the chances it was too small, and the delay came through DVE, which stood still beside POOL. The range stood on one stop with its bounds; stops at other places were in no bound, so it closed at 665.

Why so little comes back when a stop goes: PE's stops and the chain of loads and DVE work run side by side, and what PE no longer loses ahead of the seam it waits at product 2. That is the reading that fits the waits: p2 is 9.3 in the changed kernel, 9.5, 10.6 and 9.8 in banks, y_late and dve_seam, 11.8 in early6, and 14.6 in dve_seam6, where nearly all stops ahead of it are gone. The rest of T's 4 to 5 us came back at other places: in the value products (banks), in the norm (y_late), in several small waits (dve_seam). These three saved -0.8, 0.0 and 1.7. early6 saved most, and dve_seam6, which is dve_seam with early6's edit, is 6.1 us below dve_seam; why this edit gains more than the others is not shown. No variant is as fast as the kernel before; the fastest, dve_seam6r, is 2% slower (1.0198).

Left open: where the 3.2 us of PE's busy time come from that no half clock explains; by how much early6 gains (3.4 to 7.5 by itself, 6.1 on top of dve_seam), as the runs of the changed kernel scatter by 4.7 us and those of dve_seam6r by 5.6, where the kernel before scatters by 0.8; and which link sets the last 8 us ahead of product 2, where the low part's place made no difference to the time (ds6ra).
